# Experts' activations transposed by VectorE in 32 by 32 blocks, with down loads made of four runs of 32 rows

## The chip, the cores and the metric

The kernel runs on one core of a Trainium2 chip. The metric is the device time of one execution in microseconds; lower is better. The kernel before was timed three times: 1395.64, 1396.77 and 1401.73 us, with a median of 1396.77 us.

## The reference

A trunk of two layers for 256 tokens of width 1024 in float32. Layer 0 is a mixer (forgetting attention and gated linear attention) and a dense SwiGLU, layer 1 a diagonal state-space mixer and a mixture of experts. Only the experts matter here:

```
for e in range(8):                                   # two of the eight experts per token
    out = out + gates[..., e:e + 1] * swiglu(h, w_gate[e], w_up[e], w_down[e])
# swiglu(h) = (silu(h @ w_gate) * (h @ w_up)) @ w_down ; w_gate, w_up 1024 x 2816, w_down 2816 x 1024
```

The weights of the eight experts are 8 x 3 x 2816 x 1024 floats of 4 bytes, 276.8 MB, and each is read once.

## The kernel before

The program runs its stages one after another: the mixer and the dense SwiGLU of layer 0, the state-space mixer of layer 1, the routing (`route`), the experts (`experts`), and the last norm and store (`finish`). The change lies in the experts' stage alone, and in how one weight array is laid out ahead of the launch.

The routing ranks the experts by how many tokens chose them. The experts are worked off in that order and place number `e` has room for `CAPS[e]` groups of 32 tokens: `CAPS = (4, 3, 3, 3, 3, 2, 2, 2)`, 22 groups in all. A routing that doesn't fit goes through `overflow`, whose loop the data here don't enter.

The hidden width of 2816 is cut into three blocks `b`: two of 1024 and one of 768. A block has three steps:

- `gate_up(e, b)`: for each group of 32 tokens, the gathered and transposed tokens `xTs` are the weights held in TensorE (128 x 32) and the experts' gate and up matrices stream past. Four products at a time lie side by side on the four groups of 32 columns of the array (`cg(j)`), so that the product of a group of tokens comes out in a PSUM bank `gu[i]` as four bands of 32 partitions: band `j` holds 32 tokens by a quarter `j` of the block's hidden columns. ScalarE takes the silu of the gate half (L1706), VectorE multiplies it with the up half (L1707), and the result `eh` has the same four bands. In the block of 768 a third piece (L1708 to L1711) is done on 64 partitions.
- `trans(e, b)`: TensorE transposes `eh` by products with the identity (L1718, L1720, L1722), 128 x 128 at a time, into PSUM, and ScalarE or VectorE copies it into `hT` (L1724). `eh` and `hT` are two halves of one tile, so that the profile calls both `eh`.
- `down(e, b)`: 32 columns of `hT` at a time are held in TensorE and the down matrix streams past (L1731), again four at a time, and sums up over the blocks in the PSUM banks `dn`.

The order on TensorE is `gate_up(e, b)`, then `down` of the block before, then `trans(e, b)`; a queue of small jobs (gather of the next expert's tokens L1594, scatter of the last one's results L1652) is worked off between loads by `run_queue`. So `hT` of a block is read only after the next block's `gate_up`.

The weights come in units of 512 KB, 128 partitions x 1024 floats: 16 units for gate and up in a block of 1024, 12 (`o_exp_rest`, laid out ahead of the launch) in the block of 768, and 8 or 6 `down` units. One expert is 44 gate and up units and 22 down units; the eight are 528 loads. `Stream` issues them all from the queue of SyncE, in the order in which TensorE will take them, each as soon as one of 36 buffers is free (`raw`, `hT_hi`, `hT_lo`, `rawh`, `rawi`, `rawa`: L171). The buffer is given back when TensorE has used it. A down unit before is 128 rows of the down matrix that follow each other in memory:

```
r0 = D * b + 128 * f
self.unit(self.ins["o_exp_down"][0], e, slice(r0, r0 + 128))   # -> "o p d -> p (o d)", 128 x 1024
```

Of the kernel before, what the change touches and what calls it, by code (L numbers as in the profile page):

```python
# [12 lines left out]
AF = mybir.ActivationFunctionType  # L13
OP = mybir.AluOpType
AX = mybir.AxisListType

D = 1024
# [3 lines left out]
NE = 8  # L21
# [11 lines left out]
CAPS = (4, 3, 3, 3, 3, 2, 2, 2)  # L33


def make_consts():
    c = np.zeros((128, N_CONST), np.float32)
    p = np.arange(128)
    c[:, C_ID:C_ID + 128] = np.eye(128)
    c[:, C_ONE:C_ONE + 128] = 1.0  # L40
    c[:, C_CAUS:C_CAUS + 128] = np.where(p[None, :] <= p[:, None], 0.0, NEG)
    c[:, C_TRI:C_TRI + 128] = (p[:, None] < p[None, :])
    c[:, C_IOTA:C_IOTA + 128] = p[None, :] + 1
    s = (p % 32)[:, None]
    t = np.arange(32)[None, :]
    for i, l in enumerate(LEVELS):
        if l == 0:
            m = s == t
        else:
            m = (s // (2 * l) == t // (2 * l)) & (s % (2 * l) < l) & (t % (2 * l) >= l)  # L50
        c[:, C_LVL + 32 * i:C_LVL + 32 * i + 32] = m
    for hp in range(4):
        for base in (0, 32):
            c[base + 2 * hp, C_SEL + hp] = 1.0
            c[64 + base + 2 * hp + 1, C_SEL + hp] = 1.0
    m1 = ((p // 32) % 2 == 0)
    c[:, C_M1] = m1
    c[:, C_M1 + 1] = ~m1
    c[:, C_M1 + 2] = -1.0 * ~m1
    c[:, C_CAP:C_CAP + 8] = 32.0 * np.array(CAPS)  # L60
    c[:, C_LOW:C_LOW + 64] = np.tril(np.ones((8, 8)), -1).reshape(64)
    return c
# [14 lines left out]
def layout(inputs):  # L77

    r = {n: np.ascontiguousarray(inputs[n]) for n in _INS}
    col = lambda v: v.reshape(-1, 128).T  # L80
    c = make_consts()
    c[:, C_C:C_C + 8] = col(inputs["c"])
    r["consts"] = c
    r["vecs"] = np.concatenate([inputs[m.replace("mod", "norm")].reshape(-1, 128) for m in NORMS]
                               + [inputs[m + "_b"].reshape(-1, 128) for m in NORMS])
    s = np.zeros((128, N_SMALL), np.float32)
    w = inputs["e_w_in"][0]
    s[:, S_SW:S_SW + 192] = np.concatenate([w[:, 1536:1544], w[:, 3080:3096]], axis=1).reshape(8, 128, 24) \
        .transpose(1, 0, 2).reshape(128, 192)
    s[40:56, S_W2:S_W2 + 256] = inputs["e_gla_w2"][0]  # L90
    for i in range(4):
        s[32 * i:32 * i + 8, S_FB] = inputs["e_fox_fb"].reshape(8)
    s[:, S_B2:S_B2 + 2] = col(inputs["e_gla_b2"])
    s[:, S_GN:S_GN + 128] = inputs["e_gla_norm"].reshape(1, 128)
    r["smalls"] = s

    st = lambda z: z.reshape(32, 2, 64).transpose(1, 2, 0).reshape(128, 32)
    dt = np.broadcast_to(inputs["o_log_dt"].reshape(32, 2, 1), (32, 2, 64))
    d = np.zeros((128, 32), np.float32)
    d[96:128] = inputs["o_d_skip"].reshape(32, 32).T  # L100
    r["s5par"] = np.concatenate([st(inputs["o_lam_re"]), st(inputs["o_lam_im"]), st(dt), d], axis=1)
    b = [inputs[n].reshape(32, 2, 64, 16).transpose(1, 2, 0, 3).reshape(128, 512) for n in ("o_b_re", "o_b_im")]
    c = [inputs[n].reshape(32, 2, 16, 64).transpose(1, 3, 0, 2).reshape(128, 512) for n in ("o_c_re", "o_c_im")]
    r["s5bc"] = np.concatenate(b + c, axis=1)


    z = np.stack([inputs["o_exp_gate"][0], inputs["o_exp_up"][0]], axis=2).reshape(NE, NCH, 128, 2, FF)
    z5 = z[..., 2 * D:2 * D + 512].reshape(NE, NCH, 128, D)
    z2 = z[..., 2 * D + 512:].reshape(NE, 4, 2, 128, 512).transpose(0, 1, 3, 2, 4).reshape(NE, 4, 128, D)
    r["o_exp_rest"] = np.concatenate([z5, z2], axis=1)  # L110
    return r

# [130 lines left out]
class Trunk:  # L243
# [1415 lines left out]
    def experts(self):  # L1659


        nc, ex, st, mm = self.nc, self.ex, self.st, self.nc.tensor.matmul
        do = lambda n, fn, *args: self.queue.append([n, lambda: fn(*args)])
        hid = ex.tile([128, 2, 4, 256], F32, name="eh", tag="z", bufs=2)
        eh, hT = hid[:, 0], hid[:, 1]
        cg = lambda j: slice(32 * j, 32 * j + 32)
        bank = lambda n: self.psum.tile([128, 512], F32, name=n, tag=n, bufs=1)
        gu, dn = [bank(f"gu{i}") for i in range(4)], [bank(f"dn{i}") for i in range(2)]
# [10 lines left out]
        def gate_up(e, b):  # L1679
            xT = self.xT[e]  # L1680
            def wide(o):
                def emit(i, k, raw):
                    for j in range(4):
                        mm(gu[i][cg(j), o:o + 256], xT[:, k, cg(i)], raw[:, 256 * j:256 * j + 256],  # L1684
                           start=(o == 0 and k == 0), stop=(o > 0 and k == NCH - 1))
                return emit

            def rest(i, u, raw):
                for h in range(2):
                    for j in range(4):  # L1690
                        w = raw[:, 512 * h + 128 * j:512 * h + 128 * j + 128]
                        if u < 8:
                            mm(gu[i][cg(j), 128 * h:128 * h + 128], xT[:, u, cg(i)], w, start=(u == h == 0),  # L1693
                               stop=False)
                        else:
                            mm(gu[i][cg(j), 256:384], xT[:, 2 * u - 16 + h, cg(i)], w, start=False,
                               stop=(u == 11 and h == 1))

            if b < 2:
                for n, o in (("o_exp_gate", 0), ("o_exp_up", 256)):  # L1700
                    group(e, [(n, e, b, k) for k in range(NCH)], wide(o))
            else:
                group(e, [("rest", e, b, k) for k in range(12)], rest)
            for i in range(CAPS[e]):
                w = 256 if b < 2 else 128
                nc.scalar.activation(eh[:, i, 0:w], gu[i][:, 0:w], AF.Silu)  # L1706
                nc.vector.tensor_tensor(out=eh[:, i, 0:w], in0=gu[i][:, w:2 * w], in1=eh[:, i, 0:w], op=OP.mult)  # L1707
                if b == 2:  # L1708
                    o = eh[64:128, i, 128:256]
                    nc.scalar.activation(o, gu[i][0:64, 256:384], AF.Silu)  # L1710
                    nc.vector.tensor_tensor(out=o, in0=gu[i][64:128, 256:384], in1=o, op=OP.mult)  # L1711

        def trans(e, b):
            for x in range(0, CAPS[e], 2):
                n = min(2, CAPS[e] - x)
                p = self.ps([128, 2, 256])
                for i in range(n):
                    nc.tensor.transpose(p[:, i, 0:128], eh[:, x + i, 0:128], self.ident)  # L1718
                    if b < 2:
                        nc.tensor.transpose(p[:, i, 128:256], eh[:, x + i, 128:256], self.ident)  # L1720
                    else:
                        nc.tensor.transpose(p[:, i, 128:192], eh[64:128, x + i, 128:256], self.ident[64:128, 64:128])  # L1722
                w = 256 if b < 2 else 192
                (nc.vector.tensor_copy if x else nc.scalar.copy)(hT[:, x:x + n, 0:w], p[:, :n, 0:w])  # L1724

        def down(e, b):
            n = 8 if b < 2 else 6
            def emit(i, f, raw):
                c = (128 * (f % 2) + 32 * (f // 2)) if b < 2 else 32 * f
                for j in range(4):  # L1730
                    mm(dn[i // 2][cg(j), 256 * (i % 2):256 * (i % 2) + 256], hT[:, i, c:c + 32],  # L1731
                       raw[:, 256 * j:256 * j + 256], start=(b == f == i % 2 == 0),
                       stop=(b == 2 and f == n - 1 and (i % 2 == 1 or i == CAPS[e] - 1)))

            group(e, [("down", e, b, f) for f in range(n)], emit)
# [257 lines left out]
                    self.down_units(*((e, b - 1) if b else (e - 1, 2)))  # L1993
        self.down_units(NE - 1, 2)

    def unit(self, w, p, *at):

        if p not in self.place:
            self.place[p] = self.nc.values_load(self.ci[0:1, p:p + 1], min_val=0, max_val=NE - 1,
                                                engines=[mybir.EngineType.SP],  # L2000
                                                skip_runtime_bounds_check_because="a rank of the eight experts")
        w = w[(bass.ds(self.place[p], 1),) + at]
        return w.rearrange("o p d -> p (o d)")

    def down_units(self, e, b):
        for f in range(8 if b < 2 else 6):
            r0 = D * b + 128 * f
            self.st.add(("down", e, b, f), lambda e=e, r0=r0: self.unit(self.ins["o_exp_down"][0], e,
                                                                        slice(r0, r0 + 128)), "raw")


    def build(self):
# [187 lines left out]
```

## Time and profile before

| what | value |
|---|---|
| median of three runs | 1396.77 us |
| profiled execution | 1397.26 us |
| its span, first to last instruction | 1395.5 us |
| TensorE busy (matmul) | 1260.5 us, 90% |
| VectorE busy | 604.8 us, 43% |
| ScalarE busy | 380.6 us, 27% |
| mean granted TensorE clock | 0.952 |
| read from memory over the span | 394.67 MB |

All numbers but the median come from one profiled execution. Busy shares are means over stages with different limits, so they are read with a view of the stage in question. PE is TensorE's products and PEld its weight loads, DVE is VectorE, ACT ScalarE, SPq the queue of SyncE from which the loads are issued. [...]

### The profile page before, as it was taken

How to read it: one execution, taken by the hardware profiler on the slowest of the kernel's cores; microseconds unless marked ns; L12 is line 12 of the kernel's file. 1: busy time of each engine (PE TensorE's matmuls, PEld its weight loads, DVE VectorE, ACT ScalarE, POOL GpSimd, SP SyncE). 2: the span in 40 equal slices, each digit the busy share in tenths (PEclk: the TensorE clock that was granted, in tenths of full speed). 3: DMA queues.
4: the chain of work that ended last, by engine and by line, in shares of the span. 5: the costliest groups of instructions: out<-in, count | busy, mean ns of one | idle time of the engine just before them, and what ended most of it. 6: DMA issues, size and time to landing. Idle time of an engine off the chain costs nothing. (4 is left out here: it accounts for less than half of the span.)

```text
span 1395.5 us, 42895 instructions
## 1 busy us (share of the span) xinstructions
PE 1260.5 (90%) x18767; PEld 958.3 (69%) x18767; DVE 604.8 (43%) x1023; ACT 380.6 (27%) x832; POOL 264.7 (19%) x329
## 2 busy tenths in 40 slices
PE   5998988788897789989989999999999999999985
PEld 4976787777785689885676676576576585757452
DVE  6998888877789685742000210210200302111113
ACT  4455433445543475620010010110010010101001
POOL 1000122999979343000000000000000000000000
PEclk9999999889999797989999999999999999999997
DMA  9876658666786221319998989989989989999994
GB/s 343 279 224 222 197 178 265 224 219 220 228 280 201 80 73 46 107 72 407 407 395 300 373 316 354 401 300 362 393 277 383 380 305 399 407 407 406 407 404 186
DMA packets 138723, 398.59 MB, mean 286 GB/s; under 512 B 12288, under 2 KB 45312, under 8 KB 138400
## 3 DMA queue, kind: packets, MB, share of 16 engines
q1 hardware_dynamic: 138176, 394.62, 78.1%
q8 instruction: 149, 2.44, 0.7%
q0 software_dynamic: 208, 1.15, 0.3%
q14 instruction: 46, 0.38, 0.1%
q10 hardware_dynamic: 144, 0.00, 0.0%
HBM read 394.67 MB, written 1.05 MB: 284 GB/s over the span
## 5 line engine op out<-in xcount | busy, mean ns | idle before, releaser
L1707 DVE TENSOR_TENSOR eh<-gu,eh 128x256 f32<-128x256 f32 (+1 forms) x66 | 25.1, 380 | 433.1 <-ACT eh L1706 432.5
L280 PE MATMUL ps<-hT_hi,hl 128*128 128x256 f32 x576 | 172.6, 300 | 12.9 <-DVE hT_hi L433 5.5
L205 DVE TENSOR_TENSOR hl<-raw,hl 128x1024 fp32r<-128x1024 f32 x121 | 158.7, 1317 | 54.7 <-ACT hl L198 54.4
L282 PE MATMUL ps<-hT_hi,hl 128*128 128x256 f32 x576 | 169.8, 295 | 7.3 <-DVE hl L205 7.2
L281 PE MATMUL ps<-hT_lo,hl 128*128 128x256 f32 x576 | 170.0, 295 | 3.0 <-DVE hT_lo L840 2.5
L1684 PE MATMUL gu<-raw,xTs 128*32 128x256 f32 x3032 | 169.3, 380 | 1.3 <-DMA raw<-in_o_exp_up_dram 0.9
L385 POOL TENSOR_TENSOR ss<-ss 128x1 f32<-128x1 f32 x10 | 2.7, 274 | 866.0 <-ACT ps L378 784.8
L198 ACT ACTIVATE hl<-raw 128x1024 fp32r<-128x1024 f32 x121 | 126.6, 1057 | 144.6 <-DMA raw<-in_e_ffn_down_dram 29.6
L1684 PEld LDWEIGHTS gu<-raw,xTs 128*32 128x32 f32 x3032 | 96.7, 110 | 68.5 <-DMA raw<-in_o_exp_up_dram 3.4
L280 PEld LDWEIGHTS ps<-hT_hi,hl 128*128 128x128 f32 x576 | 116.3, 202 | 16.2 <-DVE hT_hi L433 5.9
L1731 PE MATMUL dn<-raw,eh 128*32 128x256 f32 x2032 | 119.0, 380 | 4.3 <-issue 3.0
L282 PEld LDWEIGHTS ps<-hT_hi,hl 128*128 128x128 f32 x576 | 116.1, 202 | 9.5 <-DVE hl L205 9.4
L281 PEld LDWEIGHTS ps<-hT_lo,hl 128*128 128x128 f32 x576 | 116.2, 202 | 5.1 <-DVE hT_lo L840 3.4
L1731 PEld LDWEIGHTS dn<-raw,eh 128*32 128x32 f32 x2032 | 68.2, 110 | 48.6 <-issue 6.9
L1706 ACT ACTIVATE eh<-gu 128x256 f32<-128x256 f32 (+1 forms) x66 | 23.0, 348 | 269.3 <-PE gu L1684 239.4
L1724 ACT COPY eh<-ps 128x512 f32<-128x512 f32 (+1 forms) x24 | 13.2, 550 | 234.0 <-PE ps L1720 155.1
L1684 PE MATMUL gu<-rawh,xTs 128*32 128x256 f32 x992 | 56.1, 380 | 0.6 <-DMA rawh<-in_o_exp_up_dram 0.6
L1724 DVE COPY eh<-ps 128x256 f32<-128x256 f32 (+3 forms) x15 | 6.8, 451 | 109.9 <-PE ps L1722 55.8
L1693 PE MATMUL gu<-raw,xTs 128*32 128x128 f32 x1664 | 49.9, 274 | 1.8 <-DMA raw<-in_o_exp_rest_dram 1.7
L1630 DVE TENSOR_TENSOR y<-dn,gate 32x256 f32<-32x256 f32 x88 | 36.9, 419 | 32.2 <-PE dn L1731 30.9
L1693 PEld LDWEIGHTS gu<-raw,xTs 128*32 128x32 f32 x1664 | 44.5, 110 | 4.7 <-DMA raw<-in_o_exp_rest_dram 3.0
L1684 PE MATMUL gu<-rawi,xTs 128*32 128x256 f32 x848 | 47.5, 379 | 0.0
(427 smaller groups left out, 2234.8 us busy)
## 6 DMA issues: line engine op xcount, KB each, us to landing
raw<-in_o_exp_down_dram SPq DMA_DIRECT2D x92, 512.0 KB, 9.2
raw<-in_o_exp_gate_dram SPq DMA_DIRECT2D x68, 512.0 KB, 6.5
raw<-in_o_exp_up_dram SPq DMA_DIRECT2D x67, 512.0 KB, 6.6
raw<-in_o_exp_rest_dram SPq DMA_DIRECT2D x58, 512.0 KB, 10.1
rawi<-in_o_exp_down_dram SPq DMA_DIRECT2D x30, 512.0 KB, 6.9
rawh<-in_o_exp_down_dram SPq DMA_DIRECT2D x27, 512.0 KB, 6.4
raw<-in_e_mod_ffn_w_dram SPq DMA_DIRECT2D x24, 512.0 KB, 4.6
raw<-in_o_mod_mix_w_dram SPq DMA_DIRECT2D x24, 512.0 KB, 4.5
```

The costliest lines, as they stand in the source:

```text
L198: nc.scalar.activation(hi, raw, AF.Copy)
L205: nc.vector.tensor_tensor(out=lo, in0=raw, in1=hi.bitcast(F32), op=OP.subtract)
L280: mm(out, lh, rh, start=start, stop=False)
L281: mm(out, lh, rl, start=False, stop=False)
L282: mm(out, ll, rh, start=False, stop=stop)
L1630: self.nc.vector.tensor_tensor(out=self.y[32 * i:32 * i + 32, cs], in0=self.dn[i // 2][js, o:o + 256], in1=self.gate[js, cs], op=OP.mult)
L1684: mm(gu[i][cg(j), o:o + 256], xT[:, k, cg(i)], raw[:, 256 * j:256 * j + 256], start=(o == 0 and k == 0), stop=(o > 0 and k == NCH - 1))
L1693: mm(gu[i][cg(j), 128 * h:128 * h + 128], xT[:, u, cg(i)], w, start=(u == h == 0), stop=False)
L1706: nc.scalar.activation(eh[:, i, 0:w], gu[i][:, 0:w], AF.Silu)
L1707: nc.vector.tensor_tensor(out=eh[:, i, 0:w], in0=gu[i][:, w:2 * w], in1=eh[:, i, 0:w], op=OP.mult)
L1724: (nc.vector.tensor_copy if x else nc.scalar.copy)(hT[:, x:x + n, 0:w], p[:, :n, 0:w])
L1731: mm(dn[i // 2][cg(j), 256 * (i % 2):256 * (i % 2) + 256], hT[:, i, c:c + 32], raw[:, 256 * j:256 * j + 256], start=(b == f == i % 2 == 0) ...
```

## The change

VectorE transposes `eh` into `hT` itself, in blocks of 32 by 32, one instruction for each group of 32 tokens. The transposes on TensorE, their PSUM tiles and the copies out of PSUM are gone. A block of 32 by 32 stays in its band: after it, 32 columns of `hT` hold, in band `j`, 32 hidden columns of quarter `j`. So the rows of the down matrix that meet them aren't 128 rows in sequence but four runs of 32 rows, 256 rows apart in a block of 1024 (128 and 64 apart in the block of 768), and `down_units` loads just these: the pattern of the source has a first dimension of 4 runs, then 32 rows, then 1024 floats. To fit this, the third piece of the block of 768 is laid out so that it lies on all 128 partitions with 64 columns.

```
-    z2 = z[..., 2 * D + 512:].reshape(NE, 4, 2, 128, 512).transpose(0, 1, 3, 2, 4).reshape(NE, 4, 128, D)
+    z2 = z[..., 2 * D + 512:].reshape(NE, 4, 2, 128, 2, 4, 64).transpose(0, 1, 3, 2, 5, 4, 6).reshape(NE, 4, 128, D)
...
-                    o = eh[64:128, i, 128:256]
-                    nc.scalar.activation(o, gu[i][0:64, 256:384], AF.Silu)
-                    nc.vector.tensor_tensor(out=o, in0=gu[i][64:128, 256:384], in1=o, op=OP.mult)
+                    o = eh[:, i, 128:192]
+                    nc.scalar.activation(o, gu[i][:, 256:320], AF.Silu)
+                    nc.vector.tensor_tensor(out=o, in0=gu[i][:, 320:384], in1=o, op=OP.mult)
 
         def trans(e, b):
-            for x in range(0, CAPS[e], 2):
-                n = min(2, CAPS[e] - x)
-                p = self.ps([128, 2, 256])
-                for i in range(n):
-                    nc.tensor.transpose(p[:, i, 0:128], eh[:, x + i, 0:128], self.ident)
-                    if b < 2:
-                        nc.tensor.transpose(p[:, i, 128:256], eh[:, x + i, 128:256], self.ident)
-                    else:
-                        nc.tensor.transpose(p[:, i, 128:192], eh[64:128, x + i, 128:256], self.ident[64:128, 64:128])
-                w = 256 if b < 2 else 192
-                (nc.vector.tensor_copy if x else nc.scalar.copy)(hT[:, x:x + n, 0:w], p[:, :n, 0:w])
+
+            w = 256 if b < 2 else 192
+            for i in range(CAPS[e]):
+                nc.vector.transpose(hT[:, i, 0:w], eh[:, i, 0:w])
...
-                c = (128 * (f % 2) + 32 * (f // 2)) if b < 2 else 32 * f
+                c = 32 * f
...
+        if rows:
+            return w.rearrange("o (j r) d -> (o j) r d", j=4)[:, rows[1]:rows[1] + 32, :]
         return w.rearrange("o p d -> p (o d)")
...
     def down_units(self, e, b):
+
         for f in range(8 if b < 2 else 6):
-            r0 = D * b + 128 * f
-            self.st.add(("down", e, b, f), lambda e=e, r0=r0: self.unit(self.ins["o_exp_down"][0], e,
-                                                                        slice(r0, r0 + 128)), "raw")
+            w = 256 if b < 2 else 128 if f < 4 else 64
+            r0, c = (D * b, 32 * f) if f < 4 or b < 2 else (D * b + 512, 32 * (f - 4))
+            self.st.add(("down", e, b, f), lambda e=e, r0=r0, w=w, c=c: self.unit(
+                self.ins["o_exp_down"][0], e, slice(r0, r0 + 4 * w), rows=(w, c)), "raw")
```

On VectorE, in the first block of the second expert and after it, the order before was as follows. `gu` are the PSUM banks of gate and up, `ps` a PSUM tile, `dn` the banks of the down product, and both halves `eh` and `hT` are called `eh`:

```order
L1707 TENSOR_TENSOR eh<-gu_6285,eh 128x256
L1707 TENSOR_TENSOR eh<-gu_6286,eh 128x256
L1707 TENSOR_TENSOR eh<-gu_6287,eh 128x256
L1724 COPY eh<-ps_8060 128x256
L1630 TENSOR_TENSOR y<-dn_6289,gate 32x256 x8
L1630 TENSOR_TENSOR y<-dn_6290,gate 32x256 x8
```

At the same place VectorE now has three transposes where the copy was:

```order
L1707 TENSOR_TENSOR eh<-gu_6285,eh 128x256
L1707 TENSOR_TENSOR eh<-gu_6286,eh 128x256
L1707 TENSOR_TENSOR eh<-gu_6287,eh 128x256
L1717 STREAM_TRANSPOSE eh<-eh 128x256 x3
L1630 TENSOR_TENSOR y<-dn_6289,gate 32x256 x8
L1630 TENSOR_TENSOR y<-dn_6290,gate 32x256 x8
```

What is queued behind them on VectorE is the same; on TensorE the six transposes between the down products of the block before and the next gate products are taken out and nothing comes in their place.

On the queue of SyncE, where the up loads of the first expert's second block end and its first down loads begin, the order before was this (the `ISA` rows work out the address of the expert):

```order
L171 DMA rawi_6129<-in_o_exp_up_dram 128x1024
L171 ISA
L171 DMA rawi_6129<-in_o_exp_down_dram 128x1024
L171 ISA
L171 DMA rawi_6130<-in_o_exp_down_dram 128x1024
```

And now at the same place:

```order
L171 DMA rawi_6129<-in_o_exp_up_dram 128x1024
L171 ISA
L171 DMA rawi_6129<-in_o_exp_down_dram 128x1x1024
L171 ISA
L171 DMA rawi_6130<-in_o_exp_down_dram 128x1x1024
```

No load has moved in the queue: all 528 stand in the order of before. The 176 down loads have another pattern, on the side of the tile 128 x 1 x 1024 and on the side of the source 4 x 32 x 1024.

## Rows read from the trace of the kernel before

**Rows 1.** Busy by stretch: us, PE, PEld, DVE, ACT, POOL; clock, DMA share, GB/s.

```profile
595.00:620.00 25.00, 21.19 (x135) 19.97 (x133) 13.90 (x44) 5.90 (x16) 2.13 (x5) 0.85 0.00 1
620.00:650.00 30.00, 29.48 (x460) 20.29 (x464) 4.17 (x21) 2.03 (x5) 0.00 (x0) 0.90 0.97 381
622.00:628.00 6.00, 6.00 (x47) 5.53 (x50) 1.23 (x3) 1.37 (x3) 0.00 (x0) 0.65 1.00 396
628.00:634.00 6.00, 6.00 (x120) 3.60 (x112) 2.40 (x15) 0.66 (x2) 0.00 (x0) 1.00 1.03 412
...
900.00:950.00 50.00, 48.55 (x1070) 36.61 (x1059) 6.62 (x16) 6.60 (x20) 0.00 (x0) 1.00 0.91 316
...
1200.00:1360.00 160.00, 150.66 (x2918) 98.99 (x2918) 21.60 (x47) 18.19 (x49) 0.00 (x0) 1.00 1.02 406
```

**Rows 2.** Timeline of the queue of SyncE: first and last loads of the stage.

```profile
620.33 5.00 SPq L171 DMA_DIRECT2D raw<-in_o_exp_gate_dram  x8
...
1366.08 0.33 SPq L171 DMA_DIRECT2D rawh<-in_o_exp_down_dram  x1
1367.38 0.34 SPq L1772 DMA_DIRECT2D rawh<-in_final_norm_dram  x1
```

**Rows 3.** Timeline, TensorE: first products of the first, second and third expert.

```profile
626.97 24.38 PE L1684 MATMUL gu<-raw,xTs 128*32 128x256 f32 x448
...
751.56 6.68 PE L1684 MATMUL gu<-rawh,xTs 128*32 128x256 f32 x120
...
852.69 6.68 PE L1684 MATMUL gu<-raw,xTs 128*32 128x256 f32 x120
```

**Rows 4.** Waits of the queue of SyncE, 620 to 1380 us: total, times, longest.

```profile
SPq L171 <- PE gu L1684: 109.5, 149, 2.4
SPq L171 <- PE dn L1731: 91.4, 102, 2.7
SPq L171 <- DMA raw<-in_o_exp_down_dram: 30.9, 42, 1.3
```

**Rows 5.** Loads issued: engine, op, count, KB each, median us to landing.

```profile
raw<-in_o_exp_down_dram SPq DMA_DIRECT2D x92, 512.0 KB, 9.2
rawi<-in_o_exp_gate_dram SPq DMA_DIRECT2D x19, 512.0 KB, 10.1
```

**Rows 6.** Queues, 525 to 620 us: packets, MB, share of 16 engines; the loads there.

```profile
q1 hardware_dynamic: 1696, 5.24, 16.2%
...
raw<-in_o_w_o_dram SPq DMA_DIRECT2D x8, 512.0 KB, 5.1
raw<-in_o_w_glu_dram SPq DMA_DIRECT2D x2, 512.0 KB, 3.3
```

**Rows 7.** Queue of the loads over the whole span.

```profile
q1 hardware_dynamic: 138176, 394.62, 78.1%
```

**Rows 8.** Timeline, TensorE: transposes of three groups, block of 768, then of 1024.

```profile
851.31 0.33 PE L1718 MATMUL ps<-cst,eh 128*128 128x128 f32 x1
...
881.32 0.33 PE L1718 MATMUL ps<-cst,eh 128*128 128x128 f32 x1
...
882.12 13.16 PE L1684 MATMUL gu<-raw,xTs 128*32 128x256 f32 x240
```

**Rows 9.** VectorE's groups by shape, 620 to 1395 us: busy, mean ns; idle before.

```profile
L1707 DVE TENSOR_TENSOR eh<-gu,eh 128x256 f32<-128x256 f32 x44 | 18.7, 425 | 268.9 <-ACT eh L1706 268.7
L1583 DVE TENSOR_SCALAR P<-cst,rpp 128x128 f32<-128x128 f32 x16 | 3.8, 279 | 0.0
L1724 DVE COPY eh<-ps 128x512 f32<-128x512 f32 x2 | 1.4, 691 | 14.5 <-PE ps L1720 14.5
```

**Rows 10.** Timeline of the end: last down load's products, the last instruction shown.

```profile
1376.15 0.59 PEld L1731 LDWEIGHTS dn<-rawh,eh 128*32 128x32 f32 x16 [0.61 <-DMA rawh<-in_o_exp_down_dram]
...
1390.88 0.72 ACT L1890 ACTIVATE X<-zf,ss 128x512 f32<-128x512 f32 x1 [1.66 <-DVE zf L1889]
```

More of the change, by code (lines that the diff above doesn't have):

```diff
@@ L1994, in order, with unit @@
         self.down_units(NE - 1, 2)
-    def unit(self, w, p, *at):
+    def unit(self, w, p, *at, rows=None):
         if p not in self.place:
```

## The prediction

> **What bounds the kernel now.** I read the busy times by stretch first, then the timelines of the load queue and of TensorE, then the waits of the load queue, and last the counts of packets. The change touches the experts' stage only. Its first load is issued at 620.33 us and its last at 1366.08 [rows 2]; 620 to 650 us show 381 GB/s, which is 28.1 of these 30 us at 407 GB/s, so bytes flow from about 621.9 us [rows 1].
>
> The stage has two limits close together. With three groups of tokens TensorE is busy nearly all the time while the loads fall to 316 GB/s, as in 900 to 950 us [rows 1]; there the load queue waits for TensorE to give buffers back, 109.5 and 91.4 us in its two largest lines [rows 4]. With two groups, from about 1200 us, the loads run at 406 GB/s with a DMA share of 1.02, so all 16 engines are full and the loads set the pace [rows 1]. An engine that is full thus moves 407 / 16 = 25.44 GB/s, and a load of 524,288 bytes over 16 engines takes 1.29 us. Some eight loads are in flight: landing takes 10.1 us in the median of one group, 8 x 1.29 = 10.3 [rows 5], and the queue also waits for landings themselves [rows 4].
>
> How a load is cut over the engines can be counted. Between 525 and 620 us there are ten loads on this queue, eight of 128 runs of 4 KB and two of 256 runs of 2 KB, 1536 runs in all; the queue shows 1696 packets [rows 6]. The 160 over are 16 for each load. I read this as one closing packet from each engine that took part, so each load was cut over all 16. Over the span the same holds: counted from the code, the queue's 756 loads and stores have 126,080 runs, and 126,080 + 16 x 756 = 138,176, the number shown [rows 7]. In each of them the first dimension that counts is 128 on both sides, so 16 equal shares of 8 rows.
>
> **The down loads.** This is the large term. Their source has now a first dimension of 4, the tile 128. An equal cut along the first dimension of both sides is into four shares of 32 rows. The trace has no load of this kind, so its price is bounded from both sides. At one end the 32 rows are cut further, 16 engines take part, and it costs nothing. At the other, no cut is made and one engine moves the whole load. I take four, as the only cut that the first dimensions allow, just as 16 shares of 128 is the cut in every load of the rows. Where they are always the same four engines, these carry in the whole stage a quarter of 176 down loads and a sixteenth of the 352 others: 92.27 / 4 + 184.55 / 16 = 23.07 + 11.53 = 34.60 MB each. At 25.44 GB/s this is 1360 us. With 16 it is 276.8 MB at 407 GB/s, 680 us. With one engine, 92.27 + 11.53 = 103.8 MB, 4080 us.
>
> [...] No row here shows a load of four shares.
>
> Do gaps come in on the four? A down load costs them 524,288 / 4 / 25,440 = 5.15 us, another 1.29. In a block of 1024 they have 16 x 1.29 + 8 x 5.15 = 61.8 us of work, in one of 768, 12 x 1.29 + 6 x 5.15 = 46.4, together 170 us per expert. TensorE took 751.56 - 626.97 = 124.6 us for the first expert and 852.69 - 751.56 = 101.1 for the second [rows 3], and less for the later ones. So it waits for loads in every expert and gives buffers back in time. Every load in flight has its last share on the four, so with eight in flight they are never empty. The rate of a full engine has bounds: 412 GB/s in 628 to 634 us is 25.75 for each [rows 1]; 5.24 MB in 16.2% of 16 x 95 us is 21.3, where loads come singly [rows 6]. That gives 1344 and 1624 us for the 34.60 MB. The queue on the four is always full, so I take 25.44. That four busy engines beside idle ones run faster than any row shows is possible; I allow 7%, my own choice, 1271 us.
>
> [...]
>
> **The transposes.** TensorE loses 132 transposes. Three groups cost 882.12 - 881.32 = 0.80 us in a block of 1024, and 852.69 - 851.31 = 1.38 us in one of 768 [rows 3, 8], so 2.98 us per expert; four groups, by 4/3, 4.0 us. Places 0 to 4 make 4.0 + 4 x 2.98 = 15.9 us. In places 5 to 7 the loads are last already. With the loads on four engines all 15.9 us vanish in TensorE's waiting: worth nothing.
>
> VectorE gains 66 transposes, 44 of 128 x 256 and 22 of 128 x 192, and loses 15 copies. None of them is in the rows; 279 ns (128 x 128) and 691 ns (128 x 512) bound one, and 425 ns (128 x 256) is nearest [rows 9]: 66 x 0.425 = 28 us at most in a stage of 775 us in which VectorE is busy 6.6 of 50 us [rows 1]. They wait for the down products of the block before, since these still read `hT`, just where the copies waited for the transposes. Behind them stand the rows of `y` and the next block's products; `hT` is wanted only after a whole `gate_up`, 20 us or more later. Nothing is late from this. If one took ten times as long, four would be 17 us and still be hidden. ScalarE's copies go with the transposes. The third piece has as many instructions as before, of the same size: nothing.
>
> **The sum.** Start of bytes 621.9, work of the four engines 1360, about 2 for the last landing and the last unit's products: 1984 us. The end after the last landing was 1395.5 - 1376.15 = 19.4 us [rows 10]; I add 1 for a lower clock, since TensorE will be idle most of the time before it. Span 2004, and 1397.26 - 1395.5 = 1.8 us around it: 2006 us. The profiled execution was 0.5 us above the median, which changes nothing at this size.
>
> **Rivals.**
>
> 1. The cut goes on over the second dimension and all 16 engines take part, or the four change from load to load and share the work alike. Then the transposes' 15.9 us are the change: loads have room until place 5, since 680 us of them lie in a stage of 756. 1397.3 - 15.9 = 1381 us. For it: the runs are 4 KB as before and there are 128 of them. Against: all counts fit a cut along the first dimension alone. It decides from about 12 engines up: 92.27 / 12 + 11.53 = 19.2 MB, 755 us, just as long as the stage is now.
> 2. TensorE becomes the bound at its lower clock. Waiting lowers it: 0.65 in 622 to 628 us, after the broken-up routing, and 1.00 again in 628 to 634 [rows 1]. If it stayed at half, the second expert would take 202 us against 170 for the loads and the first 249; five such make 1057 against 850, so up to 207 us more: 2213. Against: with 16 units at 1.34 us each in a row TensorE regains its clock as it did at 628, and each expert has 69 us to spare.
> 3. One engine moves each down load: 622 + 4080 + 22 = 4726 us. For it: two unlike patterns might not be cut at all. Against: both have a cut in common.
>
> **Chances.** Four engines at the loads' pace 0.86 (2006 us); all 16, 0.07; TensorE at half clock 0.04; one engine 0.03. The range goes from 1271 us for the four, 1915, to a rate of 24 GB/s or some of the second rival, 2100; the first and third rivals and the slowest rates lie outside. A change under 0.5% can't be told from none here. Faster 0.06, within 0.5% 0.01 (a cut near 12 engines), slower 0.93.
>
> **What would show it.** Packets of the queue: 138,176 - 176 x 12 = 136,064 with four engines, 138,176 with 16, 135,536 with one. The DMA share over the span falls from 78.1% to about 54%, and the GB/s go up and down between 407 and 4 x 25.4 = 102 in turn. Down loads land after up to 8 x 5.15 = 41 us. TensorE's waits before the down products name down loads and come to hundreds of us; 66 STREAM_TRANSPOSE near 0.4 us have no one waiting for them. If the packets stay at 138,176 and the time still rises, the first step is wrong and the cause is elsewhere; if they fall and the time doesn't follow, the rate of the four engines is.

## The result: 2140 us against 1396, in the profile after

The changed kernel takes 2140.1 us in the median of four runs (2134.4 to 2144.6), the kernel before 1396.2 beside it: 1.532 times as long, with a 95% interval from 1.528 to 1.537. The forecast was 2006 us with a range to 2100. The direction, the place and most of the size are right; 128 us of the profiled execution (2134.4 us, span 2132.5) are not in the sum.

The packets come first, because they were to tell how a load is cut. These are the rows of the load queue and of memory on the page of the changed kernel (packets, MB, share of 16 engines' span); [rows 7] is the one of before.

```profile
q1 hardware_dynamic: 136064, 394.61, 56.8%
...
HBM read 394.67 MB, written 1.05 MB: 186 GB/s over the span
```

136,064 is the count for four engines, to the packet: 12 closing packets are gone from each of 176 down loads. The share was to be about 54%. 56.8% of 2132.5 us is 1211 us in the mean of the 16 engines; before it was 78.1% of 1395.5, 1090 us. The same bytes kept an engine busy 121 us longer in the mean, about the time that the sum lacks.

The slices of the same page show how the stage runs (granted clock in tenths, DMA share in tenths, GB/s, 53.3 us a slice; the stage begins in the twelfth).

```profile
PEclk9999988989899887778878768788775666666565
DMA  8765776832236566556456655645665565566432
GB/s 312 249 213 180 241 242 202 270 128 86 90 131 245 181 210 211 168 158 204 176 182 211 211 168 159 205 176 182 210 211 165 152 200 181 178 211 209 146 136 85
```

Who waits, by the groups of the page (busy us, mean ns, then idle before and its releaser), the rows that answer to [rows 8, 9]:

```profile
L1724 PE MATMUL dn<-raw,eh 128*32 128x256 f32 x2032 | 210.6, 572 | 302.6 <-DMA raw<-in_o_exp_down_dram 301.5
...
L1717 DVE STREAM_TRANSPOSE eh<-eh 128x256 f32<-128x256 f32 (+1 forms) x66 | 27.6, 421 | 502.1 <-PE dn L1724 502.1
```

TensorE waits 302 us before the down products of one kind of buffer alone, for down loads. VectorE's transposes took 27.6 us in all and themselves wait for TensorE; no group of the page waits for them.

The waits of the load queue from 620 us to the end (total, times, longest), against [rows 4]:

```profile
SPq L171 <- PE dn L1724: 202.1, 92, 10.2
...
SPq L171 <- DMA raw<-in_o_exp_down_dram: 104.0, 22, 6.1
```

Its longest wait for one of these loads to land was 1.3 us and is 6.1, somewhat more than one down load's turn on four engines.

Six stretches of 5 us, in the columns of [rows 1], show what the sum missed:

```profile
1410.00:1415.00 5.00, 5.00 (x100) 2.80 (x96) 0.00 (x0) 0.00 (x0) 0.00 (x0) 1.00 0.25 102
1470.00:1475.00 5.00, 5.00 (x130) 4.74 (x126) 0.00 (x0) 1.29 (x4) 0.00 (x0) 1.00 0.27 102
1505.00:1510.00 5.00, 2.65 (x24) 1.03 (x24) 1.14 (x3) 0.00 (x0) 0.00 (x0) 0.62 1.04 244
1510.00:1515.00 5.00, 0.39 (x4) 0.20 (x8) 0.00 (x0) 0.00 (x0) 0.00 (x0) 0.50 1.02 241
1530.00:1535.00 5.00, 4.44 (x76) 1.92 (x72) 0.00 (x0) 0.00 (x0) 0.00 (x0) 1.00 1.03 407
1560.00:1565.00 5.00, 1.88 (x20) 0.96 (x24) 0.00 (x0) 0.00 (x0) 0.00 (x0) 0.50 1.02 249
```

There are three states, not two. Only down loads: a share of 0.25 and 102 GB/s, so four engines at 25.5 each, as forecast. Only other loads: 1.03 and 407, as forecast. Both kinds together: 1.02 to 1.04, so all 16 engines are at work, but at 241 to 249 GB/s, 15.1 to 15.6 for each in the mean. A packet of 4 KB takes 16 x 4096 B x share / rate: 0.161 us in the first row, 0.166 in the fifth, 0.279 in the third. It is no mean of fast and slow engines: of the 298 packets of 4 KB that start in 1505 to 1510 us, all but one took 0.22 to 0.34 us by their own records in the trace. Over the whole run, 17,101 of the 83,072 packets of 4 KB took between 0.2 and 0.4 us; in the kernel before it was 1,840.

The timeline of TensorE shows the same from the receiving end (start us, us, operation, and the idle time before it): the down products of one block, one row for each of its last seven units.

```profile
1484.31 1.50 PE L1724 MATMUL dn<-rawi,eh 128*32 128x256 f32 x24 [0.62 <-DMA rawi<-in_o_exp_down_dram]
1489.40 2.79 PE L1724 MATMUL dn<-rawi,eh 128*32 128x256 f32 x24 [3.58 <-DMA rawi<-in_o_exp_down_dram]
1494.48 1.50 PE L1724 MATMUL dn<-rawi,eh 128*32 128x256 f32 x24 [2.29 <-DMA rawi<-in_o_exp_down_dram]
1499.57 2.79 PE L1724 MATMUL dn<-rawi,eh 128*32 128x256 f32 x24 [3.58 <-DMA rawi<-in_o_exp_down_dram]
1506.03 2.65 PE L1724 MATMUL dn<-rawi,eh 128*32 128x256 f32 x24 [3.68 <-DMA rawi<-in_o_exp_down_dram]
1514.61 2.79 PE L1724 MATMUL dn<-rawi,eh 128*32 128x256 f32 x24 [5.92 <-DMA rawi<-in_o_exp_down_dram]
1520.76 2.79 PE L1724 MATMUL dn<-rawa,eh 128*32 128x256 f32 x24 [3.36 <-DMA rawa<-in_o_exp_down_dram]
```

The timeline of the load queue over the same time:

```profile
1475.62 15.65 SPq L171 DMA_DIRECT2D rawi<-in_o_exp_down_dram  x3
1491.52 4.83 SPq L171 DMA_DIRECT2D rawa<-in_o_exp_down_dram  x1
1497.44 23.73 SPq L171 DMA_DIRECT2D raw<-in_o_exp_gate_dram  x8
```

As long as only down loads are under way, units arrive 5.09, 5.08 and 5.09 us apart; the forecast had 5.15. From 1497.44 the next expert's gate loads come in beside them, and the units arrive 6.46, 8.58 and 6.15 us apart. The last unit shown was issued at 1491.52 and its products began at 1520.76, 29 us later.

### The profile page after: what moved, and what is told of

Read it like the earlier page. It is cut to its first block, busy times and chain, and to the rows that moved or that the text cites. A ratio compares the mean times of both kernels' runs of the same rounds, so it can differ in the third digit from the quotient of the medians.

```text
span 2132.5 us, 42687 instructions
## 1 busy us (share of the span) xinstructions
PE 1441.0 (68%) x18635; PEld 961.3 (45%) x18635; DVE 622.4 (29%) x1074; ACT 364.7 (17%) x808; POOL 264.6 (12%) x329
## 3 DMA queue, kind: packets, MB, share of 16 engines
q1 hardware_dynamic: 136064, 394.61, 56.8%
## 5 line engine op out<-in xcount | busy, mean ns | idle before, releaser
L1724 PE MATMUL dn<-raw,eh 128*32 128x256 f32 x2032 | 210.6, 572 | 302.6 <-DMA raw<-in_o_exp_down_dram 301.5
L1684 PE MATMUL gu<-raw,xTs 128*32 128x256 f32 x3032 | 181.0, 393 | 7.6 <-DMA raw<-in_o_exp_up_dram 6.7
L1717 DVE STREAM_TRANSPOSE eh<-eh 128x256 f32<-128x256 f32 (+1 forms) x66 | 27.6, 421 | 502.1 <-PE dn L1724 502.1
L1684 PEld LDWEIGHTS gu<-raw,xTs 128*32 128x32 f32 x3032 | 95.8, 114 | 92.5 <-DMA raw<-in_o_exp_up_dram 19.0
L1724 PE MATMUL dn<-rawi,eh 128*32 128x256 f32 x672 | 64.7, 540 | 88.4 <-DMA rawi<-in_o_exp_down_dram 88.4
L1724 PE MATMUL dn<-rawh,eh 128*32 128x256 f32 x568 | 58.0, 561 | 89.4 <-DMA rawh<-in_o_exp_down_dram 89.4
L1657 DVE TENSOR_TENSOR X<-ps,X 128x512 f32<-128x512 f32 x28 | 19.4, 691 | 268.8 <-PE ps L1652 268.8
L1608 ACT ACTIVATE xTs<-ps,colo_mod_ffn,colo_mod_ffn 128x96 f32<-128x96 f32 (+2 forms) x60 | 20.7, 421 | 390.9 <-PE ps L1594 390.0
L1724 PEld LDWEIGHTS dn<-rawi,eh 128*32 128x32 f32 x672 | 24.7, 142 | 125.5 <-DMA rawi<-in_o_exp_down_dram 100.6
L1724 PEld LDWEIGHTS dn<-rawh,eh 128*32 128x32 f32 x568 | 21.0, 145 | 123.8 <-DMA rawh<-in_o_exp_down_dram 100.0
```

Of the source, the lines that this page charges most:

```text
L1608: nc.scalar.activation(o, p[:, j, :], AF.Identity, bias=sh[:, k:k + 1], scale=A[:, k:k + 1])
L1657: self.nc.vector.tensor_tensor(out=X, in0=self.sc.pop(i), in1=X, op=OP.add)
L1717: nc.vector.transpose(hT[:, i, 0:w], eh[:, i, 0:w])
```

## The experiments

The theory after this profile (W, Theory 1 below): loads cut over four engines are the whole change, and beside loads of 16 engines they slow every engine's packets. Rivals: the new transposes carry some of it, or the distance of the four runs in memory does. Each kernel was timed once, except where an interval stands; seven times of the kernel before, taken beside the first eight of these kernels, have a median of 1394.35 us and lie between 1391.5 and 1398.6.

**Loads and transposes apart.** The kernel before with nothing but the new down loads (`down_units` as in the change), TensorE's transposes kept:

```diff
+        if rows:
+            return w.rearrange("o (j r) d -> (o j) r d", j=4)[:, rows[1]:rows[1] + 32, :]
         return w.rearrange("o p d -> p (o d)")
...
```

> Kernel before with the new down loads alone (four runs of 32 rows); the transposes stay on TensorE, so the down products meet other rows than they should. Theory 1, the loads alone make the change: 2140 us as in the changed kernel, within 15, 136064 packets on the load queue, and 4 KB packets of 0.27 us where down loads run beside others. Rival, VectorE's transposes or the wait of VectorE for the down products carries the 134 us over the forecast: 2006 us.

Measured: 2134.1 us, the time of the whole change (2134.4 to 2144.6). From 1505 to 1515 us its 16 engines are full (a share of 1.02 to 1.03) at 240 to 243 GB/s, so its 4 KB packets take 0.28 us as well. Its queue:

```profile
q1 hardware_dynamic: 136064, 394.61, 56.9%
```

And the changed kernel with down loads of 128 rows in sequence again:

```diff
-                self.ins["o_exp_down"][0], e, slice(r0, r0 + 4 * w), rows=(w, c)), "raw")
+                self.ins["o_exp_down"][0], e, slice(r0, r0 + 128)), "raw")   # r0 = D*b + 128*f
```

> Changed kernel with down loads of 128 rows in sequence as before; VectorE's transposes stay, so the down products meet other rows than they should. Theory 1: the first rival's sum of the prediction, 1381 us (15.9 us of transposes off TensorE while it is the bound), 138176 packets. Rival, the transposes were hidden or VectorE now holds something up: 1397 us or more.

Measured: 1381.4 us, 0.991 of before (0.988 to 0.994). Queue and transposes:

```profile
q1 hardware_dynamic: 138176, 394.62, 78.3%
...
L1717 DVE STREAM_TRANSPOSE eh<-eh 128x256 f32<-128x256 f32 (+1 forms) x66 | 27.1, 420 | 96.3 <-PE dn L1724 95.6
```

Beside the 1394.35 us of the kernel before in the same series that is 13 us less (9 to 17 by the interval), where the first rival's sum had 15.9. So the transposes are worth about what that rival said, and the loads alone carry the loss.

**A version without the loss.** VectorE's transposes keep a row in its block of 32. Instead of gathering the down rows to match, the gate and up products take their columns in runs of 32, so that the hidden rows come out in the order of 128 down rows in sequence, and the down loads are as before:

```diff
-    mm(gu[i][cg(j), o:o + 256], xT[:, k, cg(i)], raw[:, 256 * j:256 * j + 256], ...
+    mm(gu[i][cg(j), o:o + 256].rearrange("p (f q) -> p f q", q=32), xT[:, k, cg(i)],
+       raw.rearrange("p (f j q) -> p f j q", j=4, q=32)[:, :, j, :], ...
```

> Changed kernel, but gate and up products stream their columns in runs of 32 out of four times as many, so that 128 rows in sequence of the down matrix are the ones wanted; all products as the reference has them. If a stream of 32-column runs costs TensorE nothing: as with the transposes alone, 1381 us. If the runs cost it some cycles each: 2816 gate and up products of 8 runs, for 10 ns a run 4 x 56 us side by side, so some 1400 to 1440 us.

Measured: 1379.7 us, 0.990 of before (0.987 to 0.993): a gain of 1%, small, but its interval lies clear of 1. The remaining columns are stepped in the same way (the last 256 of a block through the layout of `o_exp_rest`). The products that read their columns in runs of 32, by the groups of shapes:

```profile
L1684 PE MATMUL gu<-raw,xTs 128*32 128x256 f32 x3032 | 173.1, 379 | 4.2 <-DMA raw<-in_o_exp_up_dram 2.6 <-DMA raw<-in_o_exp_gate_dram 1.4
```

379 ns is also what the same products take in the kernel with transposes only, where the columns are in sequence.

**Distance.** Four runs 33 rows (132 KB) apart instead of 256, 128 or 64 rows:

```diff
-  slice(r0, r0 + 4 * w), rows=(w, c)
+  slice(r0, r0 + 4 * 33), rows=(33, 0)          # r0 = D*b + 32*f
```

> Changed kernel, but the four runs of 32 rows start 33 rows apart (132 KB) instead of 256, 128 or 64 rows (1 MB, 512 or 256 KB), so the down products meet other rows than they should. Theory R, the even distance of the four read streams slows all engines where down loads run beside others: packets there return to 0.16 us and the time to 2006 us. Theory W, it is the four engines beside the twelve whatever the addresses read: 2140 us, packets 0.27 us. Both: 136064 packets.

Measured: 2131.0 us with 136,064 packets, and 241 to 245 GB/s at a share of 1.03 to 1.04 from 1505 to 1515 us, so packets of 0.28 us. Theory R is out.

**How many engines.** Then the number of runs was varied, to tell what the count of engines costs by itself (N) from what the slower packets cost, and each down load was cut into four loads of 32 rows. Beside W there is a rival C: not unequal numbers, but neighbouring rows in one engine's share make the packets slow. In the changed kernel:

```diff
-   rearrange("o (j r) d -> (o j) r d", j=4)[:, rows[1]:rows[1] + 32, :]
+   rearrange("o (j r) d -> (o j) r d", j=n)[:, rows[1]:rows[1] + 128 // n, :]   # n = 2, 8, 16, later 32
...
```

> Down units made of two runs of 64 rows (products meet other rows). Count alone (N): two engines carry 92.27 / 2 + 11.53 = 57.67 MB each, 2267 us at 25.44 GB/s, 622 + 2267 + 24 = 2913 us; 138,176 - 176 x 14 = 135,712 packets. With mixing (W) up to 130 us more, 3043.

Measured: 3000.6 us, between the two numbers.

> Down units made of eight runs of 16 rows instead of four of 32 (down products meet other rows, so they are not the reference's). Count alone (N): eight engines carry 92.27 / 8 + 184.55 / 16 = 23.07 MB each, 907 us at 25.44 GB/s, 622 + 907 + 24 = 1553 us; 138,176 - 176 x 8 = 136,768 packets. Count and mixing (W: each 4 KB packet takes 0.28 us rather than 0.16 while loads of both kinds run): up to 130 us more, 1685.

Measured: 1750.9 us, above both.

> Down units made of sixteen runs of 8 rows (products meet other rows). If unequal numbers of engines are the cause (N and W): 16 engines, 138,176 packets and about 1381 us, as with 128 rows in sequence. If what slows the packets is that a share now holds neighbouring rows while the shares of the other loads are spread otherwise (C): the packets stay 138,176 and the mixed stretch still runs at about 240 GB/s, 92.27 MB at 240 and 184.55 at 407 = 837 us, 622 + 837 + 24 = 1483 us.

Measured: 1592.5 us, above both. The queues of the three, in this order:

```profile
q1 hardware_dynamic: 135712, 394.61, 39.1%
```

```profile
q1 hardware_dynamic: 136768, 394.61, 69.9%
```

```profile
q1 hardware_dynamic: 138176, 394.62, 81.7%
```

The counts are those of 2, 8 and 16 engines, so the first step of the prediction holds for all of them. But what lies above the count alone is 88 us with two engines, 128 with four, 198 with eight and 211 with sixteen (3001 - 2913, 2134 - 2006, 1751 - 1553, 1592 - 1381; the 1381 is the time with loads of 128 rows, not a sum for the loads alone). It grows where the engines become equal, and with 16 equal shares W has nothing left to slow. Theory W, four beside twelve, falls as the cause. C's sign, slow stretches at an unchanged count, came true, though its 1483 us was 109 too low. Stretches of the kernel with sixteen runs, first one with gate and up loads only, then four with down loads:

```profile
1330.00:1334.00 4.00, 3.37 (x56) 1.25 (x48) 0.00 (x0) 0.00 (x0) 0.00 (x0) 1.00 1.02 413
1336.00:1340.00 4.00, 1.08 (x18) 0.42 (x16) 0.00 (x0) 0.00 (x0) 0.00 (x0) 1.00 1.04 212
1340.00:1344.00 4.00, 2.82 (x28) 1.02 (x32) 0.00 (x0) 0.00 (x0) 0.00 (x0) 0.53 1.03 229
...
1376.00:1380.00 4.00, 1.95 (x32) 0.84 (x32) 0.00 (x0) 0.00 (x0) 0.00 (x0) 1.00 1.05 236
1380.00:1384.00 4.00, 2.13 (x20) 0.59 (x16) 0.00 (x0) 0.00 (x0) 0.00 (x0) 0.65 1.02 233
```

All 16 engines are full and move 212 to 236 GB/s. The same slow packets are here with equal shares.

```diff
+   for j in range(4):
+       b.nc.sync.dma_start(out=t[32 * j:32 * j + 32], in_=s[j])     # instead of one load of four runs
...
```

> Each down load of the changed kernel becomes four loads of 32 rows (same rows, same tile); nothing else changes. Theory W (loads cut over four engines are slow, and slow the others beside them): a load of 32 rows is cut over 16 engines by 2 rows each, four times as many closing packets, 138,176 + 176 x 48 = 146,624 packets, and the time goes back to the forecast of the first rival, 1381 us, up to 1420 if 528 more issues on the load queue count. Rival P (the pairing of the rows to partitions is what costs, whoever moves them): stays above 2000 us.

Measured: 1578.5 us and 146,624 packets: 16 engines for each small load, and still nearly 200 us above what W expected. P, with over 2000 us, missed as well: the larger part of the loss goes with the count of engines.

**Which rows a load puts side by side.** A new theory, S: a load is fast where each engine writes the partitions that it writes in a load of 128 rows, and slow where the rows are dealt out otherwise. Three kernels were to tell it from the distance and from runs as such. Sixteen runs that begin 9 rows apart:

> As the sixteen runs of 8 rows, but the runs begin 9 rows (36 KB) apart instead of 64 or 32 (products meet other rows): the whole unit lies in 144 neighbouring rows. If the distance of the runs in memory slowed the packets: back to about 1381 us. If the partitions that each engine writes do it (S): about 1592 us as before, with 220 to 240 GB/s where down loads run.

Measured: 1595.4 us, with 201 to 253 GB/s in stretches of 4 us from 1338 to 1354 us, where down loads run.

Thirty-two runs of 4 rows:

> Down units made of 32 runs of 4 rows (products meet other rows); 16 engines, 138,176 packets in any case. If any pattern in runs is slow: about 1592 us or more. If what counts is that each engine keeps to the partitions that it writes in a load of 128 rows (S), and 32 runs are dealt out like 128 rows: about 1381 us, down loads at 407 GB/s. If 32 runs are dealt as 16 are (two neighbouring runs to an engine): 1592 us, and S is not decided by this run.

Measured: 1385.1 us. Its queue, and two stretches of the stage:

```profile
q1 hardware_dynamic: 138176, 394.62, 78.1%
```

```profile
1200.00:1250.00 50.00, 49.40 (x862) 33.21 (x857) 11.30 (x25) 3.47 (x9) 0.00 (x0) 1.00 1.03 407
1250.00:1300.00 50.00, 45.37 (x923) 31.82 (x915) 5.01 (x16) 4.69 (x16) 0.00 (x0) 1.00 1.02 407
```

Sixteen and thirty-two runs have the same count of engines, packets and bytes and are both gathered; 207 us lie between them.

The kernel before, each down load cut into four of 32 rows, with no runs at all:

```diff
+   for j in range(4):                                  # down units only
+       b.nc.sync.dma_start(out=t[32 * j:32 * j + 32], in_=s[32 * j:32 * j + 32])
```

> The kernel before, TensorE transposes and all, with each down load of 128 rows in sequence cut into four loads of 32 rows in sequence: the same rows on the same partitions, 146,624 packets. If the runs (four places in memory) made the four loads of 32 rows slow: 1397 us, or up to 1420 with 528 more issues. If a load that writes only 32 partitions is slow by itself (S): about 1578 to 1590 us, down loads at some 230 GB/s.

Measured: 1587.6 us. Stretches with down loads:

```profile
1348.00:1352.00 4.00, 3.41 (x40) 1.26 (x32) 0.00 (x0) 0.00 (x0) 0.00 (x0) 0.67 1.03 241
1352.00:1356.00 4.00, 1.71 (x28) 0.65 (x20) 0.00 (x0) 0.00 (x0) 0.00 (x0) 1.00 1.05 234
...
1388.00:1392.00 4.00, 2.69 (x34) 1.15 (x31) 0.69 (x1) 0.00 (x0) 0.00 (x0) 1.00 1.04 228
```

And into two of 64 rows (the same loop over 2):

> The kernel before with each down load of 128 rows in sequence cut into two loads of 64 rows in sequence (partitions 0 to 63 and 64 to 127): 138,176 + 176 x 16 = 140,992 packets. If a load is slow because it writes few partitions (32 of 128 went at about 230 GB/s, 64 could take up to twice that): down loads at about 407 GB/s, 1397 us. If 64 neighbouring partitions can be written no faster than 32 (D): down loads again at 200 to 240 GB/s, about 1585 us. [...]

Measured: 1549.8 us, against 1395.8 for the kernel before. One stretch without down loads, then three with:

```profile
1332.00:1336.00 4.00, 3.40 (x60) 1.36 (x52) 0.00 (x0) 0.00 (x0) 0.00 (x0) 1.00 1.03 406
...
1348.00:1352.00 4.00, 3.26 (x32) 1.26 (x32) 0.85 (x2) 0.77 (x2) 0.00 (x0) 0.62 0.99 253
1352.00:1356.00 4.00, 3.50 (x40) 1.53 (x36) 0.69 (x1) 0.00 (x0) 0.00 (x0) 0.95 1.04 238
1356.00:1360.00 4.00, 2.45 (x35) 1.07 (x33) 0.69 (x1) 0.00 (x0) 0.00 (x0) 1.00 1.04 243
```

Loads of 64 partitions go at 238 to 253 GB/s, hardly faster than those of 32 (228 to 241 above), though nothing is gathered and all engines work. That speaks for D; its 1585 us was 35 too high, the other forecast of 1397 us 153 too low. Taken alone, the last two kernels leave another reading open, that smaller loads are slow for their size; but 16 runs of 8 are as slow in one load of full size (212 to 236 GB/s, 1592.5 us). All of these kernels fit S. Where the rows come from made no difference where the dealing stayed the same: four runs 132 KB or up to 1 MB apart (2131.0 and 2134.4 to 2144.6 us), 16 runs 9 or up to 64 rows apart (1595.4 and 1592.5), loads of 32 rows gathered or in sequence (1578.5 and 1587.6). But S is argued from times: no kernel varied which engine writes a row apart from which engine fetches it.

## Why the prediction was wrong: the price of a full engine

The steps that held, each by its row. The cut along the first dimension: 136,064 packets, and the counts for 2, 8 and 16 runs as well. The four engines as the bound: units 5.09 us apart, and TensorE's waits are for down loads. The worth of the transposes where the loads are as before: 13 us against 15.9; that the times agree to 1 us (1381.4 against 1381) is partly luck, since the kernel before stood at 1394.35 us there and not at 1397.3. VectorE's price: 27.6 us against 28, hidden. The end: the last unit's products begin at 2112.61 us, 19.9 before the span's end, against 19.4 + 1, by this row of TensorE's timeline. (A slip without weight: with 1271 us for the four the same sum ends at 1917, not 1915. No run shows the 7% behind the 1271, the author's own choice: with down loads alone the four moved 102 GB/s, 25.5 each.)

```profile
2112.61 1.94 PE L1724 MATMUL dn<-rawh,eh 128*32 128x256 f32 x16 [3.38 <-DMA rawh<-in_o_exp_down_dram]
```

The second rival was wrong, though its premise came true: where TensorE had sat idle 3.7 and 5.9 us ahead of a unit its granted clock was 0.62 and 0.50 (1505 to 1510 and 1510 to 1515 us), and a down product took 572 ns in the mean (380 in the kernel before). It still waited for every late unit.

The step that failed is the rate in "the queue on the four is always full, so I take 25.44". The four were busy, and an engine does move 25.4 GB/s where only down loads or only the others are under way, but 15.1 to 15.6 where both are. At 241 to 249 instead of 407 GB/s, the four lose about 0.4 of such a stretch; the first load was issued at 621.12 us, so bytes flow from some 622.7 and the work took 1490 us to the last unit, 130 more than 1360: as an estimate, 130 / 0.4 = 325 us of mixed stretches. The packets' own records bear this out: the stretches of 1 us whose median 4 KB packet took 0.2 us or more add up to 284 us (in stretches of 5 us: 325), against 4 us in the kernel before; the same count is 492 us with 16 runs of 8 and 5 with 32 runs of 4. Stretches with a DMA share under 0.2 make only 5 us, so the four were hardly ever idle. Over the whole stage the four thus moved 34.60 MB in 1490 us, 23.2 GB/s each. The prediction's list of signs had named this step: if the packets fall and the time doesn't follow, the rate is wrong. The prediction took the share of an engine's time for its rate: it asked whether the engines were idle, and never whether the packets could become longer. It had a lower bound, 21.3 GB/s, whose 1624 us would have ended at 2270 us, and then cut the range to 24 without a row for it.

What makes the packets longer is settled only in part. Shown: with all 16 engines at work, loads of 128 rows and of 32 runs of 4 go at 406 to 413 GB/s, and the stretches given above with loads of 16 runs of 8, of 32 rows and of 64 rows at 201 to 253. No row of the trace tells which engine writes which partition, and why the way the rows are dealt out should make a packet longer is not shown.

Open remains why four engines alone are not slowed (102 GB/s is 25.5 for each) while their loads slow all 16 beside them. The rows allow one reading that no run tests, a limit on the sum of some 200 to 250 GB/s as long as such loads are under way: with down loads alone, two engines move 52 GB/s (1945 to 2015 us of the kernel with two runs), four 102 and eight 185 to 194 (1360 to 1374 and 1638 to 1653 us of the kernel with eight), all below it.

## What to carry to other kernels

Ask of a load not only how many engines its first dimension gives (2, 4, 8 and 16 runs gave as many here, by the packets), but whether its rows are still dealt out as in a load of 128 rows (theory S, argued from times). By the sum the first cost some 610 us here and what the sum lacks is 130; with 16 runs of 8 by S the second costs some 200 us (1592.5 against 1385.1 with 32 runs of 4), though all 16 engines take part and no byte or packet count has changed. If a layout has to be permuted, as here, try it where TensorE reads columns (379 ns for 256, stepped or not) and leave the big loads at 128 rows. A share of busy DMA time was no rate here (1.03 went with 407 GB/s, 1.02 with 241): put GB/s beside it, stretch by stretch, and let a range reach to the bounds that were worked out.

## What the runs showed of the hardware that was not expected

- A 4 KB packet took 0.16 us or about 0.28 us with every engine busy, by which loads were under way; a DMA share of 1.03 stood for 407 GB/s in one stretch and one of 1.04 for 212 in another.
- Cutting one load of 128 rows into two of 64 rows made the whole kernel 154 us longer (1549.8 against 1395.8), and into four of 32 rows 194 (1587.6 against 1393.4), one run each.
- The instruction that issues a load lasted 4.83 us for one down load where several were under way, and 15.65 for three, against 0.33 for one and 5.00 for eight before [rows 2]; the next loads, which use all 16 engines, were issued only after it.
- A transpose in blocks of 32 x 32 of 128 x 256 float values took 443 ns and of 128 x 192 378 ns on VectorE, about as much as an elementwise product of two tiles of 128 x 256 (424 to 425 ns).
